# Order of the seven products in the mixer's pairs, decay rows loaded in twos, and the place of the SSD norm sums

## The chip, the cores and the metric

One Trainium2 chip, one core of it. The metric is the device time of one execution in microseconds, taken over several runs of the same program.

## The reference

One step of a one-layer streaming encoder over 512 prompt frames and 64 sample frames (576 columns in the kernel), width 1024, all in float32:

```python
def layer(x, lp, st):
    h = x + 0.5 * swiglu(rmsnorm(x, lp['norm_ffn1']), lp['w_ffn1_in'], lp['w_ffn1_out'])
    mix, new_st = mixer(rmsnorm(h, lp['norm_mix']), lp, st)
    h = h + mix
    h = h + 0.5 * swiglu(rmsnorm(h, lp['norm_ffn2']), lp['w_ffn2_in'], lp['w_ffn2_out'])
    return h, new_st

def mixer(u, lp, st):
    (z, xbc, dt_raw, aq, ak, av, mq, mk, mv, mo, mi, mf, gl) = split_cols(u @ lp['w_in'], IN_SIZES)
    ...   # SSD scan of 16 heads in 4 groups: decays from cumulative sums of dt * a; conv of width 4 before it
    y_ssd = rmsnorm(y.reshape(bsz, L, SSD_WIDTH).astype(u.dtype) * jax.nn.silu(z), lp['ssd_norm'])
    ...   # band attention of 8 heads; mLSTM of 4 heads with its own decay rows and stabiliser
    merged = (g_ssd * (y_ssd @ lp['w_proj_ssd']) + g_att * (y_att @ lp['w_proj_attn'])
              + g_ml * (y_ml @ lp['w_proj_mlstm']))
    return merged @ lp['w_out'], (k_new, v_new, ssd_new, conv_new, c_new, n_new, m_new)
```

The RMS norm of `y_ssd` needs the sum of squares over all 1024 SSD channels of a frame.

## The kernel before

The kernel has three parts: a first feed-forward part, the mixer, and a second feed-forward part. A large share of all weight columns is multiplied in pairs of column tiles: two 128-column tiles of a weight against the 1024 x 576 activations, the activations cut into four quarters and the weights into four blocks. A pair takes seven products of half depth instead of eight (a scheme of Strassen's kind). The products are named by their operands: X1, A11, X3, X4, A22, A21, X2. A product is 4 steps of depth, each with three matmuls of 288 columns (high part by high part, high by low, low by high: `product`, L500 to 506), so 12 matmuls on line 505. There are 91 pairs, 35 of them in the mixer.

`stationary` (L415) makes the seven weight operands of a pair. Four blocks come from memory: a pair of blocks `wx` on SyncE's queue, onto which a second load on GpSimd's queue adds (L431), and three blocks `wr`. GpSimd makes two sums more (`wy`: x3 on L434, x4 on L439). Each operand is then split into a high part on ScalarE (`ph`, L251) and the rest on VectorE (`pl`, L252). The rings hold 6 `ph`, 6 `pl`, 5 `wr`, 2 `wx` and 2 `wy`.

`pair` (L447, mixer) and `swiglu_unit` (L508, feed-forward) issue the products. In the mixer three PSUM banks serve all pairs, and the next pair starts one bank further (`pair_step` is 1), so its banks `pa`, `pb`, `pc` are this pair's `pb`, `pc`, `pa`. In `pair` X1, X3, A22 and X2 add up on `pa`, A11 stands alone on `pb`, X4 and A21 add up on `pc`. Partial results are read between products: `v` (after X1, L469), `u` (after X3, L474) and `m6` (after X4, L477) are copied by ScalarE into three `uv` tiles. The four results leave through `emit`: those of A11, A22 and A21 on VectorE (L462), that of X2 on ScalarE (L460), with the nonlinear function on ScalarE behind VectorE's (L464). The next product on a bank has to wait for the read before it.

In the mixer the loop of `branches` (L1186, over `ORDER`) goes through twelve units: four attention units `a`, four mLSTM units `m` and four SSD units `s`, in the order a0 a1 m0 s0 a2 a3 s1 m1 s2 m2 s3 m3. From the third unit on each first issues the pairs of its own input columns, then one or two pairs of gate columns (`merge_gates`), then its branch work (`attn`, `ml`, `ssd`).

The decay rows (24 rows of 576 in the scratch tensor `scr_rows`) are broadcast to all partitions by loads on ScalarE's queue into tiles 2 to 7 of `R1`, which `b()` (L144) hands out in turn. An mLSTM unit takes two: `nmB` (read early, L815, L833) and `eiB` (read until the last state update, L854). Half an SSD unit takes three: `cum[0]` and `cum[1]` (loaded on L958; read by L968, L971, L993, then turned into weights by L995 to L998) and `ec` (two loads of 64 partitions on L961, read late, L999 and L1035).

After the loop the sums of squares of the SSD outputs, gathered in `self.ss`, are totalled over partitions by matmuls (`total`, L277), raised to -1/2 on GpSimd (L269), spread by matmuls again (`spread`, L293) and copied to `rs` by ScalarE. `merge` (L1061) then projects attention, mLSTM and SSD outputs in this order; `rs` is used for the last of them.

Instructions are written in the source's order, but the framework places them on the five engines' queues itself: it keeps dependencies, and among what its own timing model calls ready it prefers what stands earlier in the source. Every queue then runs in order and waits by semaphores.

## Time and profile before

| what | us |
|---|---|
| median of 3 runs | 2030.58 |
| lowest and highest run | 2024.3 and 2036.96 |
| the profiled execution, whole | 2030.21 |
| the profiled execution, span from first to last instruction | 2028.4 |
| TensorE busy | 1941.9 |
| VectorE busy | 1363.5 |
| ScalarE busy | 1033.7 |
| GpSimd busy | 631.9 |

The mean granted clock of TensorE is 0.978 of full speed. Matmuls are pipelined, so that two or three records overlap and a busy TensorE need not be at its peak; the distance from one start to the next tells the pace. Loads and other DMA issues are instructions of the queue that issues them, but are not counted as busy.

### The profile page before, as it was taken

The page shows a single profiled execution, that of the slowest core. Times are in us where ns is not written, and L with a number is a line of the kernel's source. Part 1 is how long each engine was busy: PE and PEld are TensorE (multiplying, and loading weights), DVE is VectorE, ACT ScalarE, POOL GpSimd, SP SyncE. Part 2 cuts the span into 40 slices and gives each one's busy share as a digit, 9 for nine tenths or more (in the row PEclk, how much of TensorE's full clock was granted, in tenths as well). Part 3 has the DMA queues.
Part 4 walks back from the last instruction along what each step waited for, and adds up shares of the span by engine and source line. Part 5 has one row for each costly group of instructions (what it writes and reads, how often), then busy time and mean ns, then how long its engine had stood idle before and what let it go on. Part 6 is the DMA issues. An engine that isn't in the chain of part 4 may idle for free.

```text
span 2028.4 us, 37734 instructions
## 1 busy us (share of the span) xinstructions
PE 1941.9 (96%) x14177; PEld 1877.0 (93%) x14177; DVE 1363.5 (67%) x2475; ACT 1033.7 (51%) x2188; POOL 631.9 (31%) x626
## 2 busy tenths in 40 slices
PE   9899999999999889899897998899999999999998
PEld 8899999999999669779897898799999999999998
DVE  7866656666669867667676674565686666666665
ACT  4545444544545576766766755233554544454453
POOL 5223222232202234324434353261132322222221
PEclk9899999999999899999999999899999999999999
DMA  6345445544644435645656567562234644564441
GB/s 191 89 124 161 126 125 140 156 115 126 158 123 128 119 103 148 187 128 146 177 133 166 148 172 231 159 185 87 77 95 128 164 124 126 141 157 115 126 117 66
DMA packets 127840, 278.19 MB, mean 137 GB/s; under 512 B 14225, under 2 KB 26129, under 8 KB 127657
## 3 DMA queue, kind: packets, MB, share of 16 engines
q1 hardware_dynamic: 100648, 201.74, 30.3%
q0 software_dynamic: 16304, 59.52, 16.0%
q10 hardware_dynamic: 10704, 14.52, 2.5%
q8 instruction: 112, 1.84, 0.4%
q14 instruction: 72, 0.58, 0.1%
HBM read 255.16 MB, written 20.56 MB: 136 GB/s over the span
## 4 chain that ended last, share of the span: by engine, by line
PE 47%; DMA 5%; ACT 2%; POOL 2%; issue 2%; DVE 2%; POOLq 0%; DVEq 0%; ACTq 0%
PE acc L505 25%; PE acc L223 19%; DMA R<-scr_rows 2%; DMA wx<-in_sblk 2%; DMA y<-ys 1%; ACT ph L251 1%; PE ps_s L748 0%; DVE pl L252 0%; PE ps_v L759 0%; POOL R L997 0%; POOL wy L439 0%; PE ps_x L736 0%; PE ps_s L1008 0%; POOL wy L434 0%; ACT L464 0%
## 5 line engine op out<-in xcount | busy, mean ns | idle before, releaser
L505 PE MATMUL acc<-TH,ph 128*128 128x288 f32 x2548 | 768.7, 302 | 31.9 <-DVE g L462 9.7
L505 PE MATMUL acc<-TL,ph 128*128 128x288 f32 x2548 | 760.6, 299 | 3.4 <-DVE TL L252 3.4
L505 PE MATMUL acc<-TH,pl 128*128 128x288 f32 x2548 | 758.8, 298 | 0.4 <-DVE pl L252 0.4
L251 ACT CAST ph<-wr 128x512 fp32r<-128x512 f32 x495 | 306.3, 620 | 469.8 <-PE acc L223 202.3
L505 PEld LDWEIGHTS acc<-TH,ph 128*128 128x128 f32 x2548 | 484.0, 190 | 46.2 <-DVE g L462 11.7
L505 PEld LDWEIGHTS acc<-TH,pl 128*128 128x128 f32 x2548 | 485.8, 191 | 4.6 <-issue 3.9
L505 PEld LDWEIGHTS acc<-TL,ph 128*128 128x128 f32 x2548 | 485.3, 190 | 4.5 <-DVE TL L252 3.6
L223 PE MATMUL acc<-YH,ph 128*128 128x320 f32 (+1 forms) x1536 | 455.1, 298 | 9.3 <-ACT YH L251 4.5
L252 DVE TENSOR_TENSOR pl<-wr,ph 128x512 fp32r<-128x512 f32 x495 | 373.7, 756 | 133.5 <-ACT ph L251 122.6
L223 PE MATMUL acc<-YL,ph 128*128 128x320 f32 (+1 forms) x1536 | 455.8, 298 | 2.6 <-DVE YL L302 2.2
L223 PE MATMUL acc<-YH,pl 128*128 128x320 f32 (+1 forms) x1536 | 452.9, 297 | 0.0
L223 PEld LDWEIGHTS acc<-YH,ph 128*128 128x128 f32 x1536 | 292.1, 191 | 10.8 <-ACT YH L251 4.7
L223 PEld LDWEIGHTS acc<-YL,ph 128*128 128x128 f32 x1536 | 292.6, 191 | 4.3 <-DVE YL L302 3.1
L223 PEld LDWEIGHTS acc<-YH,pl 128*128 128x128 f32 x1536 | 291.8, 191 | 0.1
L434 POOL TENSOR_TENSOR wy<-wx,wr 128x512 f32<-128x512 f32 x91 | 127.3, 1399 | 494.1 <-DVE pl L252 172.1
L252 DVE TENSOR_TENSOR pl<-wx,ph 128x512 fp32r<-128x512 f32 x182 | 159.8, 879 | 54.6 <-ACT ph L251 51.4
L431 POOL DMA_DIRECT2D wx<-in_sblk x91 | 80.5, 888 | 351.8 <-DMA wx<-in_sblk 133.5
L252 DVE TENSOR_TENSOR pl<-wy,ph 128x512 fp32r<-128x512 f32 x182 | 144.5, 795 | 66.7 <-ACT ph L251 65.6
L566 DVE SCALAR_TENSOR_TENSOR R<-acc,R 128x256 f32<-128x256 f32 (+1 forms) x256 | 116.0, 453 | 90.4 <-PE acc L223 87.1
L251 ACT CAST ph<-wy 128x512 fp32r<-128x512 f32 x182 | 112.4, 619 | 122.4 <-PE acc L223 63.8
L251 ACT CAST ph<-wx 128x512 fp32r<-128x512 f32 x182 | 112.6, 619 | 110.1 <-PE acc L505 74.6
L439 POOL TENSOR_TENSOR wy<-wy,wr 128x512 f32<-128x512 f32 x91 | 136.1, 1495 | 30.8 <-DMA wr<-in_sblk 15.1
(296 smaller groups left out, 2255.9 us busy)
## 6 DMA issues: line engine op xcount, KB each, us to landing
wr<-in_sblk SPq DMA_DIRECT2D x273, 256.0 KB, 2.7
wr<-in_wblk SPq DMA_DIRECT2D x222, 256.0 KB, 3.1
wx<-in_sblk SPq DMA_DIRECT2D x91, 512.0 KB, 3.7
wx<-in_sblk POOLq DMA_DIRECT2D x91, 512.0 KB, 5.6
R<-scr_rows ACTq DMA_DIRECT2D x24, 288.0 KB, 4.5
gs<-g SPq DMA_DIRECT2D x24, 288.0 KB, 4.2
y<-gs POOLq DMA_DIRECT2D x24, 288.0 KB, 3.7
y<-ys POOLq DMA_DIRECT2D x16, 288.0 KB, 3.3
```

Of the source, the lines that this page charges most:

```text
L223: nc.tensor.matmul(ps[:, :n], wt[:, wsl], xx[:, k0 + k, a:a + n], start=(k == 0 and i == 0), stop=(k == nk - 1 and i == 2))
L251: self.nc.scalar.copy(hi, src)
L252: self.nc.vector.tensor_tensor(lo, src, hi.bitcast(F32), op=ALU.subtract)
L431: nc.gpsimd.dma_start(x12, src[:, 1:3, :], accum_op=ALU.add)
L434: nc.gpsimd.tensor_tensor(x3, x12[:, 0, :], a22, op=ALU.add)
L439: nc.gpsimd.tensor_tensor(x4, x3, a21, op=ALU.add)
L505: self.nc.tensor.matmul(ps, wt[:, wsl], xx[:, t, kk, :], start=(start and kk == 0 and i == 0), stop=(kk == 3 and i == 2), skip_group_check ...
L566: nc.vector.scalar_tensor_tensor(x[:, ot, sl], ps, 0.5, x[:, ot, sl], op0=ALU.mult, op1=ALU.add)
```

## The change

The diff has four parts.

- In `pair` the order of the products becomes X1, X4, then X2 of the pair before, X3, A21, A11, A22; X2 is kept as `open_pair` and issued by the next pair (or by `pair_end` before the last unit). `pa`, `pc`, `pb` are the first, second and third bank now. The operands are split in the order of `MUSE` in the mixer.
- `stationary` writes all loads first, then both sums, then the splits. In the feed-forward parts the order of the splits (`FUSE`) is the one of before; in the mixer the block for A11 is loaded last.
- `b()` hands out the six tiles in two groups of three and loads two rows with one DMA. An mLSTM unit leaves its third tile unused.
- The output DMA of the convolution rows (`co`), the totals of the SSD sums and their spread move from behind the loop to a place ahead of the last unit's branch work.

```diff
-    def b(self):
+    def b(self, step, r0):
+        i = 2 + self.b_i % 2 * 3
         self.b_i += 1
-        return self.R1[:, 2 + (self.b_i - 1) % 6, :]
+        self.nc.scalar.dma_start(self.R1[:, i:i + 2, :], self.rows(r0, 128, step))
+        return [self.R1[:, i + j, :] for j in range(3)]
...
+    FUSE = (T_X1, T_A11, T_X3, T_X4, T_A22, T_A21, T_X2)
+    MUSE = (T_X1, T_X4, T_X3, T_A21, T_A11, T_A22, T_X2)
...
         x12 = self.ring("wx", shape=(128, 2, 512))
         nc.sync.dma_start(x12, src[:, 0:2, :])
         nc.gpsimd.dma_start(x12, src[:, 1:3, :], accum_op=ALU.add)
-        a11, a22 = load(0), load(2)
-        x3 = self.ring("wy")
-        nc.gpsimd.tensor_tensor(x3, x12[:, 0, :], a22, op=ALU.add)
-        out[self.T_X1] = self.parts(x12[:, 0, :])
-        out[self.T_A11] = self.parts(a11)
-        a21 = load(3)
-        x4 = self.ring("wy")
-        nc.gpsimd.tensor_tensor(x4, x3, a21, op=ALU.add)
-        out[self.T_X3] = self.parts(x3)
...
+        for q in (2, 3, 0) if self.mixer else (0, 2, 3):
+            load(q)
+        raw["x3"] = add(x12[:, 0, :], raw[2])
+        raw["x4"] = add(raw["x3"], raw[3])
...
+        return {t: self.parts(at[t]) for t in (self.MUSE if self.mixer else self.FUSE)}
...
-        pa, pb, pc = self.pair_banks()
+        pa, pc, pb = self.pair_banks()
...
         self.product(pa, ops, self.T_X1, True)
-        v = tmp()
-        nc.scalar.activation(v, pa, AF.Copy, scale=s1)
+        v = tmp(pa, s1)
+        self.product(pc, ops, self.T_X4, True)
+        m6 = tmp(pc, s2)
+        self.pair_end()
+        self.product(pa, ops, self.T_X3, False)
+        u = tmp(pa, s2)
+        self.product(pc, ops, self.T_A21, False)
+        put2(1, H[1], emit(pc, s2, u, ALU.subtract))
         self.product(pb, ops, self.T_A11, True)
         put1(1, H[1], emit(pb, s1, v, ALU.add))
-        self.product(pa, ops, self.T_X3, False)
-        u = tmp()
-        nc.scalar.activation(u, pa, AF.Copy, scale=s2)
-        self.product(pc, ops, self.T_X4, True)
-        m6 = tmp()
-        nc.scalar.activation(m6, pc, AF.Copy, scale=s2)
         self.product(pa, ops, self.T_A22, False)
         put2(0, H[0], emit(pa, -s2, m6, ALU.add))
-        self.product(pc, ops, self.T_A21, False)
-        put2(1, H[1], emit(pc, s2, u, ALU.subtract))
-        self.product(pa, ops, self.T_X2, False)
-        put1(0, H[0], emit(pa, s1))
+
+        def end():
+            self.product(pa, ops, self.T_X2, False)
+            put1(0, H[0], emit(pa, s1))
+        self.open_pair = end
+
+    def pair_end(self):
+        end, self.open_pair = self.open_pair, None
+        if end:
+            end()
...
-    def rows(self, r0, n):
-        return bass.AP(self.scr.tensor, self.scr.offset + r0 * T, [[0, n], [1, T]])
+    def rows(self, r0, n, step=0):
+        return bass.AP(self.scr.tensor, self.scr.offset + r0 * T, [[0, n]] + [[step * T, 2]] * bool(step) + [[1, T]])
...
-        nmB, eiB = self.b(), self.b()
-        nc.scalar.dma_start(nmB, self.rows(16 + h, 128))
-        nc.scalar.dma_start(eiB, self.rows(20 + h, 128))
+        nmB, eiB, _ = self.b(4, 16 + h)
...
-            cum = [self.b(), self.b()]
-            for r in range(2):
-                nc.scalar.dma_start(cum[r], self.rows(d0 + r, 128))
-            ec = self.b()
+            *cum, ec = self.b(1, d0)
...
+                if n == len(ORDER) - 1:
+                    self.pair_end()
+                    nc.sync.dma_start(self.O["co"], self.co)
+                    for (a, m), acc in zip(HALVES, self.ss):
+                        pt = self.ps("x")
+                        self.total([acc], m, pt)
+                        nc.scalar.copy(self.rs[:, a:a + m], self.spread(pt, m)[0][:, :m])
                 units[u[0]][1](u[1], t)
                 if n == GATES:
                     self.gates(pre)
-            nc.sync.dma_start(self.O["co"], self.co)
-            for (a, n), acc in zip(HALVES, self.ss):
-                pt = self.ps("x")
-                self.total([acc], n, pt)
-                nc.scalar.copy(self.rs[:, a:a + n], self.spread(pt, n)[0][:, :n])
```

## Rows read from the trace of the kernel before

**Rows 1.** The page: its first line, and shares of the chain that ended last.

```profile
span 2028.4 us, 37734 instructions
...
PE acc L505 25%; PE acc L223 19%; DMA R<-scr_rows 2%; DMA wx<-in_sblk 2%; DMA y<-ys 1%; ACT ph L251 1%; PE ps_s L748 0%; DVE pl L252 0%; PE ps_v L759 0%; POOL R L997 0%; POOL wy L439 0%; PE ps_x L736 0%; PE ps_s L1008 0%; POOL wy L434 0%; ACT L464 0%
```

**Rows 2.** Busy time by stage: from:to length, per engine busy us (instructions), clock, DMA.

```profile
core 0: us, PE busy (x) PEld busy (x) DVE busy (x) ACT busy (x) POOL busy (x), PEclk, DMA share, GB/s
100.00:600.00 500.00, 500.00 (x3759) 500.00 (x3758) 320.96 (x537) 227.41 (x436) 125.06 (x105) 1.00 0.51 138
640.00:1257.00 617.00, 564.82 (x3991) 508.62 (x3991) 436.41 (x907) 411.64 (x985) 245.46 (x258) 0.96 0.56 152
1257.00:1294.00 37.00, 24.00 (x108) 20.50 (x108) 14.21 (x33) 10.12 (x29) 11.98 (x21) 0.68 0.58 186
...
1530.00:2000.00 470.00, 470.00 (x3537) 469.95 (x3536) 300.85 (x486) 208.52 (x396) 115.57 (x98) 1.00 0.47 128
```

**Rows 3.** TensorE's waits, 640 to 1257: us, times, longest us.

```profile
PE acc L505 <- DVE g L462: 9.7, 4, 3.7
PE acc L505 <- ACT g L460: 8.9, 3, 5.5
PE acc L505 <- ACT uv L474: 4.5, 4, 3.6
...
PE acc L505 <- ACT P L460: 2.0, 1, 2.0
```

**Rows 4.** Busy time, as rows 2, of two stretches at the lower clock.

```profile
1280.00:1291.40 11.40, 6.51 (x26) 6.33 (x27) 3.21 (x10) 1.66 (x3) 5.24 (x9) 0.50 0.53 180
1030.50:1033.90 3.40, 3.40 (x17) 3.40 (x16) 3.40 (x11) 2.12 (x6) 0.73 (x2) 0.50 0.45 154
```

**Rows 5.** ScalarE in order of time, 1240 to 1249: start, us, what.

```profile
1240.08 0.40 ACT L477 ACTIVATE uv<-acc 128x288 f32<-128x288 f32 x1
...
1243.26 0.40 ACT L469 ACTIVATE uv<-acc 128x288 f32<-128x288 f32 x1
...
1246.85 0.40 ACT L460 ACTIVATE g<-acc 128x288 f32<-128x288 f32 x1
...
1248.49 0.41 ACT L474 ACTIVATE uv<-acc 128x288 f32<-128x288 f32 x1
```

**Rows 6.** VectorE in order of time, 1241 to 1246.

```profile
1241.30 0.46 DVE L462 SCALAR_TENSOR_TENSOR g<-acc,uv 128x288 f32<-128x288 f32 x1
...
1244.86 0.46 DVE L462 SCALAR_TENSOR_TENSOR g<-acc,uv 128x288 f32<-128x288 f32 x1 [0.78 <-PE acc L505]
```

**Rows 7.** Pieces of the chain that ended last, in order of time: start, us.

```profile
820.33 1.60 PE acc L505 x12
...
1102.43 4.88 DMA R<-scr_rows
```

**Rows 8.** ScalarE and its queue in order of time, 1096 to 1117.

```profile
1096.22 0.33 ACTq L958 DMA_DIRECT2D R<-scr_rows  x1
...
1102.43 0.32 ACTq L958 DMA_DIRECT2D R<-scr_rows  x1
...
1115.67 0.40 ACT L460 ACTIVATE g<-acc 128x288 f32<-128x288 f32 x1
```

**Rows 9.** DMA issues, 640 to 1300: count, KB each, median us to landing.

```profile
wr<-in_sblk SPq DMA_DIRECT2D x99, 256.0 KB, 3.0
wx<-in_sblk SPq DMA_DIRECT2D x35, 512.0 KB, 3.6
```

**Rows 10.** GpSimd in order of time, at 1253, with the idle time before it.

```profile
1253.36 0.89 POOL L431 DMA_DIRECT2D wx<-in_sblk  x1 [8.38 <-DVE pl L252]
```

**Rows 11.** VectorE at 1133 and GpSimd at 1174, in order of time.

```profile
1133.73 0.34 DVE L854 SCALAR_TENSOR_TENSOR cs<-cs,R,ps_s 128x129 f32<-128x129 f32 x1
...
1174.74 6.39 POOL L997 TENSOR_TENSOR R<-R,t 128x512 f32<-128x512 f32 x4
```

**Rows 12.** TensorE in order of time, 1280 to 1292.

```profile
1280.18 1.01 PE L277 MATMUL ps_x<-ones,sumsq 128*128 128x1 f32 x4 [0.53 <-DVE g L884]
...
1291.44 1.05 PE L293 MATMUL ps_x<-ident,sm 128*128 128x128 f32 x4
```

More of the change, by code (lines that the diff above doesn't have):

```diff
@@ L77, in __init__ @@
         self.b_i = 0
+        self.open_pair = None
         nc = self.nc
@@ L421, in stationary, with add @@
         src = self.I["sblk"][i].rearrange("p (q c) -> p q c", q=4)
+        raw = {}
         def load(q):
-            w = self.ring("wr")
-            nc.sync.dma_start(w, src[:, q, :])
-            return w
-        out = {}
+            raw[q] = self.ring("wr")
+            nc.sync.dma_start(raw[q], src[:, q, :])
+        def add(one, two):
+            o = self.ring("wy")
+            nc.gpsimd.tensor_tensor(o, one, two, op=ALU.add)
+            return o
         x12 = self.ring("wx", shape=(128, 2, 512))
@@ L431, in stationary @@
         nc.gpsimd.dma_start(x12, src[:, 1:3, :], accum_op=ALU.add)
[L432 to L445 removed]
+        for q in (2, 3, 0) if self.mixer else (0, 2, 3):
+            load(q)
+        raw["x3"] = add(x12[:, 0, :], raw[2])
+        raw["x4"] = add(raw["x3"], raw[3])
+        at = {self.T_X1: x12[:, 0, :], self.T_X2: x12[:, 1, :], self.T_X3: raw["x3"], self.T_X4: raw["x4"],
+              self.T_A11: raw[0], self.T_A22: raw[2], self.T_A21: raw[3]}
+        return {t: self.parts(at[t]) for t in (self.MUSE if self.mixer else self.FUSE)}
     def pair(self, one, two):
@@ L452, in pair, with tmp @@
         ops = self.stationary((name, c1, c2))
-        pa, pb, pc = self.pair_banks()
+        pa, pc, pb = self.pair_banks()
         H = (slice(0, FH), slice(FH, T))
-        tmp = lambda: self.gp.tile([128, FH], F32, name="uv", tag="uv", bufs=3)
+        def tmp(ps, scale):
+            o = self.gp.tile([128, FH], F32, name="uv", tag="uv", bufs=3)
+            nc.scalar.activation(o, ps, AF.Copy, scale=scale)
+            return o
         def emit(ps, scale, other=None, op=None):
```

5 lines of the change are left out of this document (removed).

## The prediction

> **What bounds the kernel now.** I read the busy time by stage first. In the feed-forward parts TensorE is busy every microsecond (500.00 of 500.00, 470.00 of 470.00) at full clock; nothing that the change does to weights or copies there can be seen unless it makes TensorE wait. The mixer, 640 to 1257 us, is different: 564.82 of 617.00 us busy, and the clock was granted at 0.96 on average. Behind it, 1257 to 1294, TensorE works 24 of 37 us at a clock of 0.68, since the last mLSTM unit ends there alone [rows 2]. So about 52 us of idle time and a few per cent of clock in the mixer are the stock that the change can draw on. Of this, the waits of product matmuls (L505) for a copy out of PSUM are, in their four largest rows, 9.7 + 8.9 + 4.5 + 2.0 = 25.1 us in 12 waits, the longest 5.5 us [rows 3]. After five of these waits the clock fell to 1.2 GHz for some 3.4 us; one stands, 0.50 over 3.40 us [rows 4]. Each such stretch costs half of itself, 1.7 us, together 8.5 us. The other waits of the mixer belong to the branches (softmax, states, norms), which the change does not touch.
>
> The chain that ended last names, beside products, the loads of the decay rows: 2% of the span [rows 1].
>
> **Which order runs today.** The new order shall put more work between a copy and the product that needs its bank. Whether it does depends on the order that runs, and that is not the order of the source. The source puts X2 of a pair before X1 of the next. On ScalarE, however, the copy of X4 (L477, 1240.08) is followed by that of the next pair's X1 (L469, 1243.26), and only then by that of X2 (L460, 1246.85) and of the next X3 (L474, 1248.49) [rows 5]. Between them lie on VectorE the copies of A22 (1241.30) and A21 (1244.86) [rows 6]; A21 adds onto X4's bank and so can't have run before that bank's copy had ended at 1240.48 and 1.60 us more had gone by. So TensorE runs X4, A22, X1', A21, X2, X3', A11', X4', A22': the next pair's first product has already been pulled forward. This is so at 29 of the 34 borders of two mixer pairs (L469 of the next before L460 of this one), of which the border in [rows 5] is the last. Counted on the three banks, every copy there has two products behind which to hide: X1 to X3 (A21, X2), X3 to A22 (A11, X4), X4 to A21 (A22, X1'), A22 to X2 (X1', A21), and X2, A21 and A11 to the next user of their bank likewise. The new source order X1, X4, X2 of the pair before, X3, A21, A11, A22 gives each copy two products as well. A product is 12 matmuls in 1.60 us [rows 7], so the cover is 3.2 us before and after.
>
> **The change part by part.**
> *Interleave.* Same 35 pairs, same seven products, same copies, same weight splits. Gain at the usual borders: none; at the five others one product of cover at most, 1.60 us each. Bounds: 0 and 22 us (the first rival). I take 0, by [rows 5, 6], the rows nearest to it. The first weight sum now needed early (X4 second) is no new wait so long as GpSimd keeps its lead; the splits run through the same six buffers. The moved X2 keeps its split two products longer, which leaves A22 of the next pair a lead of three products, 4.8 us. In the feed-forward parts only the order in which weight work is written changes; TensorE's full stages hide it, and without that cover it would cost at most a product per stage.
> *Decay rows.* Twelve loads of 288 KB fewer, as many bytes. Each issue takes ScalarE's queue 0.33 us [rows 8], 4 us in all, hidden since ScalarE is busy 411.64 of 617.00 us [rows 2]. Twice the bytes land later: 3.0 us for 256 KB and 3.6 us for 512 KB [rows 9], so the first row comes 0.6 us later. The gain is where the second row was asked for late. In the last SSD unit the loads were issued at 1096.22 and 1102.43, the second took 4.88 us on the chain [rows 7, 8], and ScalarE, late by this and by table loads, reached the copy L460 only at 1115.67 [rows 8]: this is the longest wait of all, 5.5 us [rows 3], and it dropped the clock. One load brings the second row 6.21 - 0.6 = 5.6 us sooner. That ends the wait and its slow stretch: 5.5 + 1.7 = 7.2 us. There is a catch in the buffers. Groups of three make the second half of an SSD unit behind an mLSTM unit load its rows into the two buffers of that unit, whose second one is read until the last state update (L854, 1133.73), while today only the late-needed third tile waits for it. The load moves some 30 us later there; its product on GpSimd (L997) starts at 1174.74 [rows 11], so this is hidden, and it too takes ScalarE's work out of the crowd at 1102 to 1116. If the crowd forms again elsewhere, the gain is 0. I take 7.2.
> The row says that 256 KB more cost 0.6 us. The Trainium skill, DMA: Bandwidth & Descriptors, section Anatomy of one DMA, gives every DMA a fixed part of about 2.0 us beside its bytes; if all twelve saved loads stood on the path, that would be an estimate of 24 us, 2007 us in the end. The traces here show no such path but the case above; this result is weighed among the rivals.
> *Norm sums.* Twenty small matmuls leave the end. There four of L277 took 1.01 us and four of L293 1.05 us [rows 12], at half clock (0.50 from 1280 to 1291.4 [rows 4]), so 0.13 us each at full clock, 2.6 us for twenty. Most of them ran while TensorE waited for the last unit anyway; only about 1.1 us stood among the merge's matmuls. In their new place they lie among products: +2.6 - 1.1 = +1.5 us. The output DMA of the convolution rows moves along on SyncE's queue, one issue, hidden. After the last pair X2 now follows A22 at once and waits for its copy, 0.46 us long [rows 6]; this falls into time that the last unit leaves free.
>
> Sum, against the profiled execution's 2030.2 us (span 2028.4 [rows 1] and 1.8 around it; the median of the runs is 0.4 above): 0 - 7.2 + 1.5 = -5.7, so 2024.5; I say 2024 us.
>
> **The rivals.**
> *The interleave works.* If the order that runs gains a whole product of cover, each wait loses up to 1.60 us: 6.4 of the 9.7 (four waits), 4.8 of the 8.9 (three), 1.6 + 0.9 of the 4.5 (longest 3.6), 1.6 of the 2.0, together 15.3 us [rows 3]; four of five slow stretches go with it, 6.8 us. With what is left of the row loads' 7.2 (3.9) and +1.5 this is 2030.2 - 22.1 - 3.9 + 1.5 = 2006 us. For it: five borders still run in the poor order, and the placing then no longer hangs on guesses. Against: the two-product cover of [rows 5, 6].
> *The loads are the path.* 2% of the span is 40.6 us [rows 1]; half of the loads gone would take 20.3: 2030.2 - 20.3 + 1.5 = 2011 us. Against: twins that were issued together already overlap, and the consumers are ScalarE and VectorE, not TensorE.
> *The norm sums stall the products.* The sums need a power on GpSimd, and TensorE's queue then holds matmuls that wait for it, with products queued behind them and, behind these, every copy. GpSimd stood 8.38 us before a weight load in just this stretch [rows 10]. If the power is queued behind such a wait, once for each half, TensorE loses up to 16.8 us and two slow stretches, 3.4: 2024.5 + 20.2 = 2045 us. It makes the kernel slower than before once both waits together pass 5.7 us. For it: GpSimd's queue is in order and waits for transfers; against: nothing needs these sums at once, so they can be placed late.
> *Nothing moves.* ScalarE's crowd forms elsewhere and the sums cost little: 2030 us.
>
> **How the numbers follow.** My forecast (2014 to 2034) 0.42; the interleave works 0.26; the loads are the path 0.08; the norm sums stall 0.14; nothing 0.10. The likeliest is 2024 us. Faster by over 1% (below 2010; about 1% is what a measurement of this kernel can tell from no change) has the 0.26 and half of 0.08: 0.30. Slower by over 1% (above 2051) has the far end of the third rival: 0.06. Within: 0.64. Leaving out the lowest part of the first rival and the highest of the third, the range is 2003 to 2044 us.
>
> **What would show it.** Right: the sum of the L505 waits for copies falls by about the one long wait and not by half; ScalarE's order shows the copies of X1, X4, X2, X3 in a row; the decay rows are 12 loads of 576 KB that land in 5 us or so; the second load of the last SSD unit lies after the last state update. Wrong: L505 waits under 12 us and clock stretches gone (first rival), TensorE waiting at L293 for GpSimd between 1220 and 1257 (third). A weight split for A22 or X4 as releaser of a product would mean that the lead I counted as enough is not.

## The result, and the profile after

The changed kernel takes 2037.22 us in the median of 20 runs (2029.76 to 2046.3), the kernel before 2033.16 us in as many runs beside it (2024.3 to 2039.28). The ratio is 1.0027, with a 95% interval of 1.0015 to 1.0039: by this about 5.5 us slower, where 6 us faster had been forecast. The profiled execution has a span of 2034.0 us, against 2028.4 us [rows 1].

The first line of the page after, and busy time by stage (columns as in [rows 2]):

```profile
span 2034.0 us, 37661 instructions
```

```profile
core 0: us, PE busy (x) PEld busy (x) DVE busy (x) ACT busy (x) POOL busy (x), PEclk, DMA share, GB/s
640.00:1257.00 617.00, 561.17 (x3928) 504.19 (x3927) 427.50 (x899) 410.38 (x978) 239.56 (x256) 0.95 0.55 150
1257.00:1294.00 37.00, 22.82 (x144) 20.25 (x142) 16.76 (x34) 13.25 (x35) 11.61 (x18) 0.78 0.61 177
```

Within the same 617 us the mixer issued 3928 matmuls instead of 3991 [rows 2]. TensorE is busy 3.65 us less, and its mean clock is 0.95 instead of 0.96. The last matmul of the mixer's products starts at 1265.9 us instead of 1256.8 (rows of the product's line), so the loss is made in the mixer. The feed-forward parts were not the place: by the rows of the product the first one runs 1.6 us ahead of before from its fourth pair to its end, and the second one 5.4 to 5.5 us behind from its fourth pair to its end.

TensorE's waits for a copy, after, from 640 to 1257 (us, times, longest; L523 is the product's line now, L465 copies v, u and m6, L471 and L473 are the results on ScalarE and VectorE):

```profile
PE acc L523 <- ACT uv L465: 14.6, 9, 5.3
PE acc L523 <- ACT g L471: 6.7, 3, 4.5
PE acc L523 <- DVE g L473: 3.9, 4, 2.0
PE acc L523 <- DVE R L473: 1.2, 2, 0.6
```

These four are 26.4 us in 18 waits. Before, the product's waits for copies were 25.1 us in the four largest rows [rows 3] and 27.2 us in all. So the interleave did not take the waits away, but it did not add to them either.

ScalarE in order of time, after: four copies in the new order X1, X4, X2 of the pair before, X3, as the source has them.

```profile
1224.28 0.41 ACT L465 ACTIVATE uv<-acc 128x288 f32<-128x288 f32 x1
1225.88 0.40 ACT L465 ACTIVATE uv<-acc 128x288 f32<-128x288 f32 x1
...
1232.66 0.40 ACT L471 ACTIVATE g<-acc 128x288 f32<-128x288 f32 x1
1233.84 0.41 ACT L465 ACTIVATE uv<-acc 128x288 f32<-128x288 f32 x1
```

Before, the second of these places was held by VectorE's copy of A21, and X4 was sixth [rows 5, 6]. The decay rows come as planned (DMA issues, 640 to 1257: count, size, median us to landing):

```profile
R<-scr_rows ACTq DMA_DIRECT2D x12, 576.0 KB, 5.9
```

To see where the time goes, the mixer is cut in two in all kernels below: from the first matmul of its products to the last one, and from there to the 97th matmul of the merge (start to start), when in these two kernels all branch work is done. Idle is time with no matmul in flight; the last column but one is the time in the first stretch in which the records of the granted clock show 0.5.

| kernel | first to last product, us | idle in it | of it at 1.2 GHz | last product to the merge's 97th matmul |
|---|---|---|---|---|
| before | 612.7 | 52.2 | 44.4 | 42.9 |
| after | 623.3 | 55.8 | 61.4 | 41.4 |

After loses 10.6 us among the products: 3.6 us more idle, and 17 us more at half speed, which cost up to half of themselves, 8.5 us (the two overlap in part). At the end it gains 1.5 us. One execution of each stands behind these figures, and executions of one kernel differ by several us (the kernel before took 2017.64 to 2038.36 us in one set of 32 runs). Verdicts therefore rest on the ratios over many runs, and the traces only say where to look.

### The profile page after: what moved, and what is told of

It is laid out like the page before. It is cut to its first block, busy times and chain, and to the rows that moved or that the text cites. A ratio compares the mean times of both kernels' runs of the same rounds, so it can differ in the third digit from the quotient of the medians.

```text
span 2034.0 us, 37661 instructions
## 1 busy us (share of the span) xinstructions
PE 1940.2 (95%) x14177; PEld 1875.7 (92%) x14177; DVE 1360.7 (67%) x2475; ACT 1036.9 (51%) x2190; POOL 628.8 (31%) x626
## 3 DMA queue, kind: packets, MB, share of 16 engines
q0 software_dynamic: 16304, 59.52, 16.1%
## 5 line engine op out<-in xcount | busy, mean ns | idle before, releaser
L523 PE MATMUL acc<-TH,ph 128*128 128x288 f32 x2548 | 773.0, 304 | 29.2 <-ACT uv L465 14.6
L523 PE MATMUL acc<-TL,ph 128*128 128x288 f32 x2548 | 762.3, 299 | 3.4 <-DVE TL L256 3.4
L523 PE MATMUL acc<-TH,pl 128*128 128x288 f32 x2548 | 761.6, 299 | 0.0
L523 PEld LDWEIGHTS acc<-TH,ph 128*128 128x128 f32 x2548 | 486.5, 191 | 42.1 <-ACT uv L465 17.3
L523 PEld LDWEIGHTS acc<-TL,ph 128*128 128x128 f32 x2548 | 487.4, 191 | 5.5 <-DVE TL L256 3.6
L523 PEld LDWEIGHTS acc<-TH,pl 128*128 128x128 f32 x2548 | 488.1, 192 | 2.9 <-issue 2.2
L438 POOL TENSOR_TENSOR wy<-wy,wr 128x512 f32<-128x512 f32 x91 | 134.8, 1481 | 34.6 <-DMA wr<-in_sblk 14.8
```

The source lines that it names most:

```text
L438: nc.gpsimd.tensor_tensor(o, one, two, op=ALU.add)
L523: self.nc.tensor.matmul(ps, wt[:, wsl], xx[:, t, kk, :], start=(start and kk == 0 and i == 0), stop=(kk == 3 and i == 2), skip_group_check ...
```

## The experiments

### Each part by itself

Four kernels, each the kernel before with one part of the change. The interleave:

```diff
+    MUSE = (T_X1, T_X4, T_X3, T_A21, T_A11, T_A22, T_X2)
...
-        pa, pb, pc = self.pair_banks()
+        pa, pc, pb = self.pair_banks()
...
+        self.product(pc, ops, self.T_X4, True)
+        m6 = tmp(pc, s2)
+        self.pair_end()
```

> The kernel before with the new order of the seven products, the pair left open, and the new stationary operands; rows loaded one at a time and norm sums at the end as before. Theory A (the steps of the prediction; the order that ran before already gave every copy two products, and the loss of the changed kernel is the norm sums): no change, within 3 us of before, waits of products for copies near 27 us in the mixer. Theory B (the new order of loads and weight sums delays GpSimd's SSD work and the weights, and this is where the changed kernel lost its 10 us in pairs 57 to 62): 5 to 10 us slower. Theory C (the interleave gives each wait a product of cover, and the other parts ate this up): 10 us or more faster, copy waits under 12 us.

Measured: ratio 1.0029 (1.0016 to 1.0042), 5.9 us slower. Copy waits are 25.8 us, as theory A had it, but the time is not the same: from first to last product 626.1 us, 57.6 idle, 78.5 us of it at 1.2 GHz. Theory B gave the size; that its mechanism is the cause is not shown by this.

The rows:

```diff
-        return self.R1[:, 2 + (self.b_i - 1) % 6, :]
+        self.nc.scalar.dma_start(self.R1[:, i:i + 2, :], self.rows(r0, 128, step))
```

> The kernel before with the decay rows two per load in groups of three tiles, nothing else. Theory A: 7 us faster, since the longest wait of all (5.5 us at 1116 us, a copy on ScalarE behind the decay-row work of the last SSD unit) and its slow stretch go. Theory B: no change within 2 us; the copy is late for another reason than the second row's load and the wait of 5 us or so stays (the changed kernel has one of 5.6 us at the same place). Theory D (groups of three make row loads wait for the tile before): 3 us or more slower.

Measured: ratio 0.9954 (0.9936 to 0.9971), 9.3 us faster. That is theory A's size. But the wait that theory A was to remove is still there, and this is looked into below.

The norm sums, with the store of the convolution rows:

```diff
+                if n == len(ORDER) - 1:
+                    nc.sync.dma_start(self.O["co"], self.co)
+                    for (a, m), acc in zip(HALVES, self.ss):
+                        pt = self.ps("x")
+                        self.total([acc], m, pt)
```

> The kernel before with the store of the convolution rows and the norm sums moved ahead of the last unit, nothing else. Theory A as predicted: 1.5 us slower. Theory A as it stands after the result (the sums hold both PSUM tiles that the last unit's transposes need, and its store comes 9 us later): 6 to 10 us slower, with the transposes of the last unit at 1250 us or later in place of 1237 to 1243. Theory B: within 1.5 us, the last unit where it was.

Measured: ratio 1.0015 (1.0001 to 1.0030), 3 us slower: between 0.2 and 6 us, so the 1.5 us of the prediction are in, 6 to 10 us hardly. The last unit's store does come later, at 1287.40 us instead of 1280.35.

The weight loads and sums written first, in the old order of products:

```diff
+        for q in (0, 2, 3):
+            load(q)
+        raw["x3"] = add(x12[:, 0, :], raw[2])
+        raw["x4"] = add(raw["x3"], raw[3])
```

> The kernel before with the weight loads and sums written first in both the feed-forward parts and the mixer, in the old order of products and splits. Theory A: no change within 1.5 us; the first pair some 1.1 us earlier and the stall of 1.7 us at 1516 us may go, as in the changed kernel, so up to 3 us faster. Theory E (any rewriting lets the framework place the mixer's instructions anew, and this alone moves the time by 5 us either way): a change of 3 us or more with a different set of waits in the mixer.

Measured: ratio 1.0009 (0.9994 to 1.0024), no difference that can be told. This also answers theory E in part: a rewriting that lets the framework place instructions anew need not move the time.

The parts alone add up to 5.9 - 9.3 + 3.0 = -0.4 us (the interleave contains the rewritten loads); the whole is +5.5. Each of these figures is uncertain by some 3 us either way, so that they do not simply add is likely rather than certain. The interleave is the one with the largest price.

### What the interleave costs, and which part of it

First the changed kernel without the moved norm sums:

```diff
-                    for (a, m), acc in zip(HALVES, self.ss):
-                        pt = self.ps("x")
...
+            nc.sync.dma_start(self.O["co"], self.co)
+            for (a, n), acc in zip(HALVES, self.ss):
```

> The changed kernel without the move of the convolution rows' store and the norm sums (both behind the loop again); interleave and rows two per load stay. Theory N (the norm sums hold the PSUM tiles of the last unit's transposes and cost the changed kernel its 9 us): the store of the last unit falls back to 1280 us or sooner, 2025 us or less. Theory I (the interleave alone delays the last unit as far, and the sums add little): 2033 to 2039 us, as the interleave alone.

Measured: ratio 1.0015 (1.0000 to 1.0029). By the middle values the sums account for 0.0012, 2.4 us of the changed kernel's loss, though the two intervals overlap; theory N's 9 us are out. Then the changed kernel without the interleave:

```diff
-        self.product(pc, ops, self.T_X4, True)
-        m6 = tmp(pc, s2)
-        self.pair_end()
+        self.product(pb, ops, self.T_A11, True)
+        put1(1, H[1], emit(pb, s1, v, ALU.add))
```

> The changed kernel without the interleave: rows two per load, norm sums and store of the convolution rows moved, weight loads written first, the old order of products. Theory L (parts add up: rows -9, sums +3, the rest 0 to +2): 4 to 6 us faster than before. Theory O (rows gained by the place of the last unit on TensorE's queue, and here no product stands behind its state matmuls, as in the kernel before): no gain, 0 to 6 us slower than before.

Measured: ratio 0.9977 (0.9965 to 0.9989), 4.7 us faster than before, as adding up the parts gave it, and against theory O. With the interleave the same kernel stands at 1.0027. So the interleave costs 0.0050 in the whole, 10 us.

Is it the open pair, or the order? The order that ran before [rows 5, 6] also interleaves two pairs, but X4 is its sixth product. So this kernel writes just that order down, nothing else changed:

```diff
         self.product(pa, ops, self.T_X1, True)
         v = tmp(pa, s1)
+        self.pair_end()
         self.product(pa, ops, self.T_X3, False)
         u = tmp(pa, s2)
         self.product(pb, ops, self.T_A11, True)
         put1(1, H[1], emit(pb, s1, v, ALU.add))
         self.product(pc, ops, self.T_X4, True)
         m6 = tmp(pc, s2)
         self.product(pa, ops, self.T_A22, False)
         put2(0, H[0], emit(pa, -s2, m6, ALU.add))
+        def end():
+            self.product(pc, ops, self.T_A21, False)
+            put2(1, H[1], emit(pc, s2, u, ALU.subtract))
+            self.product(pa, ops, self.T_X2, False)
+            put1(0, H[0], emit(pa, s1))
+        self.open_pair = end
```

> The kernel before with another interleave, written in the order that already ran there: X1, then the last two products A21 and X2 of the pair before, X3, A11, X4, A22; operands split in this order, loads as before, rows one per load, norm sums at the end. Two products of cover for every copy here too, but the sums x3 and x4 of GpSimd are needed third and sixth, not fourth and second. Theory Q (the interleave of the change costs its 6 us because X4 stands second: ScalarE and GpSimd then wait for the weight sums and their accumulating load with copies queued behind; ScalarE's waits for wy and wx were 19.9 us there, 5.1 before): within 3 us of before, these waits under 9 us. Theory A2 (leaving a product open across pairs costs by itself, as the store of the last unit comes later): 4 us or more slower than before.

Measured: ratio 0.9993 (0.9979 to 1.0007), as before, and 0.0036 (7 us) below the interleave of the change. TensorE's waits for copies in it, 640 to 1257:

```profile
PE acc L519 <- ACT uv L461: 5.7, 6, 2.1
PE acc L519 <- ACT g L467: 5.5, 3, 2.0
PE acc L519 <- DVE R L469: 1.6, 2, 1.3
PE acc L519 <- DVE P L469: 1.5, 2, 0.8
PE acc L519 <- DVE g L469: 1.0, 1, 1.0
PE acc L519 <- ACT P L467: 0.8, 1, 0.8
```

16.1 us instead of 27.2: an interleave can shorten these waits, if it stands in this order. The time did not follow in this kernel, since waits of branch matmuls grew from 24.5 to 30.3 us and the time at 1.2 GHz from 44.4 to 61.4. One point of theory Q failed here, and it is the mechanism: ScalarE's waits for weights and their sums were to fall under 9 us and are 20.5 (18.3 for the accumulated load, 2.2 for GpSimd's sums), as many as with the interleave of the change (19.9).

Two more pairs of kernels differ in nothing but this order. The changed kernel in the order as it ran:

```diff
-        pa, pc, pb = self.pair_banks()
+        pa, pb, pc = self.pair_banks()
...
-        self.product(pc, ops, self.T_X4, True)
-        m6 = tmp(pc, s2)
         self.pair_end()
```

> The changed kernel with nothing but the order of its products altered: X1, A21 and X2 of the pair before, X3, A11, X4, A22 in place of X1, X4, X2 of the pair before, X3, A21, A11, A22 (weight loads and splits in this order). Theory Q (X4 as second product is what the interleave costs, 6 us alone and 10 in the whole): 8 to 13 us faster than the changed kernel, so 3 to 8 us faster than before. Theory A2 (keeping products open across pairs costs): within 3 us of the changed kernel.

Measured: ratio 0.9950 (0.9934 to 0.9965), 10 us faster than before and 0.0077, 15.6 us, faster than the changed kernel. And the best kernel (rows two per load, the last unit's branch work first, see below) in either order; this edit puts the last unit first:

```diff
-                    self.merge_gates(n - 2)
-                    if n - 2 >= len(ORDER) - 4:
+                    if n < len(ORDER) - 1:
+                        self.merge_gates(n - 2)
+                    if n - 2 >= len(ORDER) - 4 and n < len(ORDER) - 1:
                         self.merge_gates(n)
...
                 units[u[0]][1](u[1], t)
+                if n == len(ORDER) - 1:
+                    self.merge_gates(n - 2)
+                    self.merge_gates(n)
+                    self.pair_end()
```

> The interleave in the order that already ran, rows two per load, last unit's branch work ahead of its gate pairs, norm sums at the end. Theory Q with O: 5 to 12 us faster than before. Theory A2: no better than before.

> The best kernel so far (the order as it ran, rows two per load, last unit's branch work first: 0.990 of before) with only the order of products altered to that of the change, X4 second and X2 alone open. Theory Q: 7 to 12 us slower than it, so 8 to 13 us faster than before. Theory A2: no slower than it.

Measured: 0.9901 (0.9880 to 0.9922) in the order as it ran, 2012.28 us in the median; 0.9990 (0.9976 to 1.0003) with X4 second. The difference is 0.0089, 18 us. Theory Q had the sign each time and too small a size in the last three kernels: 8 to 13 us expected and 15.6 measured, 5 to 12 and 20, 7 to 12 and 18, so that the last kernel is only 2 us below before instead of 8 to 13. Theory A2 is out: keeping products open across pairs costs nothing by itself. Three times the order alone decides, and in no pair do the two intervals touch. (The order here is the whole of it, with the loads and splits that go with it; no run moves X4 alone.)

| kernel | order | ratio | first to last product | idle in it | at 1.2 GHz |
|---|---|---|---|---|---|
| interleave alone | X4 second | 1.0029 | 626.1 | 57.6 | 78.5 |
| | as it ran | 0.9993 | 610.3 | 46.7 | 61.4 |
| whole change | X4 second | 1.0027 | 623.3 | 55.8 | 61.4 |
| | as it ran | 0.9950 | 602.3 | 45.9 | 23.9 |
| rows, last unit first | X4 second | 0.9990 | 628.9 | 58.2 | 68.3 |
| | as it ran | 0.9901 | 609.5 | 47.2 | 37.5 |

Each time some 10 us of idle time and 17 to 38 us at half speed go. In each pair the products' waits for copies (640 to 1257) are shorter as well, although the cover, as written, is two products in both orders: 16.1 us instead of 25.8, 20.2 instead of 26.4, 21.8 instead of 28.1.

Why the copies come later with X4 second is not settled by these traces. The first suspect is GpSimd, whose sum x4 is needed earlier. GpSimd's waits ahead of its weight sums (us, times, longest), first the changed kernel, then the same kernel in the order as it ran:

```profile
POOL wy L438 <- DVE pl L256: 62.5, 13, 6.9
POOL wy L438 <- issue: 29.9, 6, 7.3
...
POOL wy L438 <- DMA wx<-in_sblk: 5.6, 1, 5.6
```

```profile
POOL wy L437 <- DMA wx<-in_sblk: 72.7, 15, 7.3
POOL wy L437 <- DVE pl L256: 19.1, 4, 10.9
...
POOL wy L437 <- issue: 15.3, 3, 6.5
```

By the names, the sums of the second kernel start when their weights land, and those of the first when VectorE has split an operand and so set a buffer free. The names divide the kernels by order without exception: 15, 14, 15 and 17 waits for the load in the kernel before and the three with the order as it ran; one or none in the three with X4 second. But a wait for several things is named after one of them only, and the landing times in the trace say otherwise. One of the sums of the changed kernel, with the load that it needs:

```profile
651.18 0.92 POOL L443 DMA_DIRECT2D wx<-in_sblk  x1 [1.50 <-DVE ga L645]
...
658.03 1.32 POOL L438 TENSOR_TENSOR wy<-wx,wr 128x512 f32<-128x512 f32 x1 [3.24 <-DVE pl L256]
```

The load landed at 657.90; the split that the wait is named after had ended at 657.54. Of the 35 first sums (x3) of the mixer's pairs, 32 start within 0.25 us behind the landing of their own load in the changed kernel, 31 in the same kernel in the order as it ran, 30 in the kernel before. So GpSimd starts on the load in either order, and that it lost a lead, or that its two `wy` tiles hold it up, is not shown. ScalarE's waits for weights do not part the orders either: with X4 second and as it ran they are 19.9 and 20.5 us, 17.1 and 16.7, 15.9 and 17.9 in the three pairs of the table. Only the part of them that is for GpSimd's sums is larger with X4 second: 12.6, 6.5 and 7.1 us against 2.2, 2.3 and 2.8.

How a late weight can reach a product is seen at 1195 us of the changed kernel. GpSimd in order of time, then ScalarE, then TensorE:

```profile
1177.48 6.41 POOL L1010 TENSOR_TENSOR R<-R,t 128x512 f32<-128x512 f32 x4
1183.86 2.05 POOL L1011 TENSOR_TENSOR R<-R,t 64x64 f32<-64x64 f32 x4
1185.86 0.85 POOL L443 DMA_DIRECT2D wx<-in_sblk  x1
1186.48 1.31 POOL L997 TENSOR_TENSOR t<-t,wd 128x512 f32<-128x512 f32 x1
1195.05 1.27 POOL L438 TENSOR_TENSOR wy<-wx,wr 128x512 f32<-128x512 f32 x1 [7.26 <-issue]
```

```profile
1195.01 0.62 ACT L255 CAST ph<-wx 128x512 fp32r<-128x512 f32 x1 [9.12 <-DMA wx<-in_sblk]
1195.53 0.40 ACT L471 ACTIVATE g<-acc 128x288 f32<-128x288 f32 x1
```

```profile
1195.99 0.61 PE L523 MATMUL acc<-TH,ph 128*128 128x288 f32 x1 [4.47 <-ACT g L471]
```

The accumulating load is issued behind 8.5 us of branch work on GpSimd (L1010, L1011) and lands 9.1 us later. ScalarE stands 9.12 us at the split that needs it, the copy L471 stands behind the split, and the product behind the copy. The product's wait is named after the copy, but the 3.2 us of two products could not hide it. This is one of the changed kernel's eight waits of a product of 1 us or more, 4.5 of their 21.4 us. The longest, 5.33 us at 1117.54, stands behind table loads and decay work on ScalarE, and the one of 3.66 us at 988.89 behind a late decay row. Nor is it a place where the order loses: in the order as it ran ScalarE stands 5.21 us at 1176.14 for the load of the same pair, and over the 84 matmuls around it that kernel's lead goes from 14.8 to 13.2 us. The changed kernel falls behind it at many places: by 7.5 us after eight such stretches of 84 matmuls, 17.2 after 18, 21.0 at the end. That the order is the cause is shown by the three pairs; which of its waits carries it stays open. A kernel with X4 alone moved, and one with a third `wy` tile, were not tried.

### What the rows two per load gained

The wait at 1116 us was to go. In the kernel with rows alone it is there, 5.60 us at 1114.56. ScalarE ahead of it:

```profile
1104.37 1.28 ACT L467 ACT_TABLE_LOAD   x1 [1.83 <-DVE wd L967]
...
1106.63 1.28 ACT L969 ACT_TABLE_LOAD   x1
1107.93 0.21 ACT L969 ACTIVATE el<-R 128x4 f32<-128x4 f32 x1
...
1108.44 1.28 ACT L467 ACT_TABLE_LOAD   x1
...
1110.18 1.28 ACT L971 ACT_TABLE_LOAD   x1
...
1111.59 1.50 ACT L991 ACTIVATE R<-R,TM 128x128 f32<-128x128 f32 x5
...
1114.12 0.39 ACT L477 ACTIVATE uv<-acc 128x288 f32<-128x288 f32 x1
```

Four table loads, 5.1 us, as ScalarE changes between the gate function of the results (L467) and the exponentials of the decay work (L969 and after). The same four stand there before: 1107.65, 1109.41, 1111.44 and 1113.19. The page ScalarE activation tables: per-element evaluation and per-set limits of the Trainium skill (section What a function is on this engine) puts two functions of different sets one such load of 1283 ns apart; the trace agrees, 1283 ns each. To see whether they are the cause, the kernel before, with rows one per load, and with ScalarE copying where the pairs have a gate function:

```diff
             def go(dst, a=0, b=FH, func=None):
+                func = func and AF.Copy
```

> The kernel before with the gate and sigmoid functions of the mixer's pairs left out: ScalarE copies in their place, with as many instructions of the same shape, so that it need not change its function table between them and the exponentials of the branches (46 table loads of 1.28 us in the mixer before). Theory T (the longest wait of a product, 5.5 us at 1116 us, is four table loads in a row on ScalarE, 5.1 us, ahead of the copy that the product needs; the second decay row is not what it waits for): that wait falls under 1.5 us with the rows loaded as before, and the kernel is more than 10 us faster. Theory R (the wait is the late second row's load): the wait stays above 4 us.

Measured: ratio 0.9933 (0.9909 to 0.9958), 13.6 us faster. Table loads between 640 and 1257 fall from 46 to 11, and the product's waits are short everywhere (us, times, longest):

```profile
PE acc L506 <- DVE g L463: 5.1, 5, 2.1
PE acc L506 <- ACT uv L470: 4.2, 3, 2.8
PE acc L506 <- ACT uv L475: 4.1, 5, 2.0
```

No wait of a product of 1.3 us or more lies between 1070 and 1200. Theory T is right: the wait was the table loads', not the late row's. (A branch matmul waits 4.9 us for GpSimd at 1120 instead.)

Where, then, do the 9 us come from? In the trace of rows alone the products take 5.4 us more (618.1), and the end 32.0 us instead of 42.9. The last mLSTM unit stands otherwise on TensorE's queue: its first state matmul has four products behind it, in the kernel before none. Its output is stored at 1273.57 instead of 1280.35 (SyncE's row of the store), and the merge waits for it. So two kernels asked whether the loads or this place made the gain. Groups of three tiles with one row per load:

```diff
-        self.nc.scalar.dma_start(self.R1[:, i:i + 2, :], self.rows(r0, 128, step))
+        for r in range(2):
+            self.nc.scalar.dma_start(self.R1[:, i + r, :], self.rows(r0 + r * step, 128))
```

> The kernel before with the tiles of the decay rows handed out in groups of three as in the change, but with one row per load (24 loads of 288 KB, as before). Theory L (the gain of rows alone is that of fewer, larger loads): no change from before. Theory O (the gain comes from where the framework then places the last unit's matmuls on TensorE's queue, which hangs on anything written differently): the time moves by the store of the last mLSTM unit, end = store + 746 us within 2 us, wherever that store falls; a gain as large as that of rows alone would mean the groups matter and not the loads.

Measured: ratio 1.0032 (1.0017 to 1.0046), 6.5 us slower; idle time among the products 62.4 us, a single wait for a copy 8.88 us. The store falls at 1288.04. Theory L had expected no change, so it missed the price of the groups; the end of the execution comes 748.9 us behind the store, against 748.0 in the kernel before, so theory O's link between the two holds, with a constant 2 to 3 us larger than it said. And two per load in the mLSTM units alone:

```diff
-        for r in range(2):
-            self.nc.scalar.dma_start(self.R1[:, i + r, :], self.rows(r0 + r * step, 128))
+        if step == 4:
+            self.nc.scalar.dma_start(self.R1[:, i:i + 2, :], self.rows(r0, 128, step))
+        else:
+            for r in range(2):
+                self.nc.scalar.dma_start(self.R1[:, i + r, :], self.rows(r0 + r * step, 128))
```

> Groups of three tiles as in the change; two rows per load only in the four mLSTM units, the last unit among them; one row per load in the SSD units (20 loads). On TensorE's queue the last unit stands as in the kernel before, with no product behind its states. Theory L (the last unit ends sooner since its two rows come with one load): 5 us or more faster than groups of three with single rows, so no slower than before. Theory O: as groups of three with single rows, 3 to 10 us slower than before, store at 1284 us or later.

Measured: ratio 0.9992 (0.9976 to 1.0008), 8 us faster than groups with single rows. The last unit stands as before, so theory O fails for this gain: it was made among the products (609.0 us, 51.1 idle; groups with single rows 621.1 and 62.4). Its store falls at 1274.11, where theory O had 1284 or later. Theory L gave the size, though by its mechanism the gain would stand at the end, which is 42.3 us against 43.4. So the groups cost some 6 us when the rows come singly, and loads of two give this back; the further step to rows alone shows at the end.

### The place of the last unit

The branch work of the last unit written ahead of its gate pairs (the diff stands above; `pair_end` only where a pair is open), in the kernel before, in the changed kernel, and with rows alone:

> The kernel before with one edit: the branch work of the last mLSTM unit is written ahead of its two pairs of gate columns instead of behind them; nothing of the change is in it. On TensorE's queue the unit's first state matmul then has 8.7 products behind it, in the kernel before none, with rows two per load alone 4. Theory O (what decides is where the last unit's matmuls stand among the last products): its store falls at 1270 us or sooner (before: 1280.4) and the kernel is 8 to 14 us faster than before. Theory L (fewer, larger row loads made the gain of rows alone; nothing of them is here): no gain. Rival W (TensorE then waits for the unit's copies with fewer products as cover): within 3 us or slower.

> The changed kernel with the same edit, the last unit's branch work ahead of its two pairs of gate columns (8.8 products behind its first state matmul; the changed kernel has none). Theory O: store at 1270 us or sooner (changed kernel: 1289.7), 10 to 16 us faster than the changed kernel, so 5 to 10 us faster than before. Theory P (the products in the mixer are slower by the interleave and this remains): at most 4 us faster than the changed kernel.

> The kernel before with rows two per load and with the last unit's branch work written ahead of its gate pairs; nothing else. Theory O: both put the last unit's matmuls ahead of products (here 9.6 of them behind its first state matmul, 4 with rows alone), so the gains do not add: 5 to 10 us faster than before. Theory L (a gain of the loads, 9 us, and one of the place, 6 us): 13 us or more faster.

Measured: 0.9971 (0.9948 to 0.9993), 5.9 us faster than before; 1.0019 (1.0001 to 1.0038), within 2 us of the changed kernel; 0.9960 (0.9944 to 0.9975), no more than rows alone. The end shrinks each time, to 30.3, 28.0 and 29.9 us. In the kernel before this is the gain, smaller than the 8 to 14 us expected; its store falls at 1261.02, as theory O said, and some of the unit's matmuls now lie among the products, which take 4.5 us more. With rows two per load it is a gain that rows alone had made already, so theory O is right about the end and about the sum. In the changed kernel theory O failed and theory P's size came: the end shrinks by 13.4 us, but the store still falls at 1286.03, and the products took 639.9 us in the profiled run, its slowest (2041.22, median 2034.58). There the norm sums show what they can do (TensorE's waits, 1230 to 1262):

```profile
PE ps_x L297 <- POOL sm L273: 4.9, 1, 4.9
PE ps_x L281 <- DVE sumsq L267: 2.4, 1, 2.4
```

TensorE stands 4.9 us before the spread, waiting for GpSimd's power, with products queued behind. That is the mechanism of the prediction's third rival. In the changed kernel itself only the wait for the sums (2.5 us at 1232.76) shows.

The same end from the other side: the merge loads and projects the attention outputs first, so that the gate loads no longer stand on GpSimd's queue behind the load of the last unit's output.

```diff
-        for i in range(8):
-            self.split(load(self.ys[i]), YH[:, i, :], YL[:, i, :])
         for branch, w in ((1, "w_proj_attn"), (2, "w_proj_mlstm")):
+            for i in range(4 * branch - 4, 4 * branch):
+                self.split(load(self.ys[i]), YH[:, i, :], YL[:, i, :])
```

> The changed kernel, with one edit in the merge: it loads and splits the four attention outputs, projects them, and only then loads the four mLSTM outputs (before: all eight first, so that on GpSimd's queue the gate loads of the attention part stand behind the load of the last mLSTM unit's output). Theory S (the end follows the last mLSTM unit's store, 9.4 us later in the changed kernel than before, and this is where its time went): from the merge's first matmul (1272.3 us) to its 48th (1300.6 us) lie 28.3 us; 6.4 of it are those matmuls and some 3 the last unit's own, so 15 to 19 us faster than the changed kernel, near 2020 us. Theory P (the products before the merge are what got slower, and the store is late as a consequence only): under 4 us faster.

> The kernel before with rows two per load, and the same edit in the merge. Theory S: rows alone gained 9 us since its last unit's store came 6.8 us sooner; with the store off the path 48 matmuls of the merge, which took 17.4 us there, take 6.4 and some 2 of the last unit: another 7 to 9 us, near 2013 us. Theory P: within 3 us of rows alone (2021 us).

Measured: the changed kernel goes from 1.0027 to 0.9962 (0.9945 to 0.9978), 13 us; rows alone stays, 0.9949 (0.9934 to 0.9964) against 0.9954. In both the merge then waits 6.0 and 6.4 us ahead of its mLSTM part, for outputs that are now loaded late, which gives back a part. So theory S holds for the changed kernel, where the late store was most of what stood in the merge's way, with 2 us less than it said; for rows alone, whose store was early already, theory P's size came, and what was won at the merge's start was lost again at its mLSTM part.

## Why the prediction was right or wrong

**The bound.** Right. What the change did, it did in the mixer and at its end; the forecast's stock of idle time and slow clock was the place of the gains and of the loss.

**The order that ran.** Right as a count. Two products covered a copy before and after, and waits for copies went from 27.2 to 26.4 us. What does not follow from the count is an equal time, as the next point shows. The bound kept open for the interleave, up to 22 us of gain, was no fancy either: written in the order that had run, copy waits fell to 16.1 us, and together with rows and the last unit's place the kernel reached 0.9901.

**The interleave at 0: the step that failed.** The interleave was entered with 0, because every copy keeps two products of cover, and with the sentence that a weight sum needed early "is no new wait so long as GpSimd keeps its lead". The term measured +5.9 us alone and +10 us in the whole (1.0027 against 0.9977). The mistake was to take equal cover for equal time: two orders with the same cover of two products differ by 7, 15.6 and 18 us in three pairs of kernels, and the waits for copies in them by 6 to 10 us. Products were moved, and so were the times at which their operands must be ready and their copies taken: X4 from sixth to second place is four products or 6.4 us earlier [rows 7], for an operand that takes an accumulating load, two sums and a split. No price was put on this. That GpSimd lost its lead by it is not shown, since its first sums start on the landing of their load in either order (32 and 31 of 35), so through which wait the order costs its time stays open.

**The slow clock.** The forecast charged each wait its half-speed stretch, and this was right in kind: of the 10.6 us lost among the products up to 8.5 are clock. But it charged the product's waits alone. Waits of branch matmuls were left out, as work that the change does not touch, and those grew from 24.5 to 29.0 us.

**Decay rows.** Right in sign and, alone, in size (-7.2 forecast, -9.3 measured, interval -13.0 to -5.9); wrong in mechanism. The wait of 5.5 us was four table loads; it outlived the change (5.3 us at 1117.54 there). The working had named table loads beside the late row and then given the whole wait to the row. The gain came elsewhere: loads of two gave back what the groups cost with single rows, and the rest shows at the end, with the last unit's other place. With the interleave in place it was 0.0014 (1.0029 to 1.0015), 3 us, with intervals that overlap. The load's size was about right: 576 KB land in 5.9 us, 288 KB in 4.5 before (24 loads). The fixed part of the Trainium skill's DMA: Bandwidth & Descriptors, section Anatomy of one DMA, which that section gives for loads that GpSimd issues, would make an estimate of 24 us over twelve loads; no run here shows that for these loads on ScalarE's queue.

**Norm sums.** +1.5 us forecast, +2.4 in the whole and +3.0 alone (0.2 to 6.1). Right in sign, low by a us or so: TensorE's wait for the sums was not in the working.

**The sum.** 0 - 7.2 + 1.5 became, as it added in the whole, +10 for the interleave and -4.7 for all the rest (1.0027 and 0.9977). One term, entered as nothing, turned the sign. The measured 2037 us lies in the range, since that reached to 2044 for the third rival; the mechanism that took it there was for the most part not the one for which that end was kept, so that was luck.

**What was to show it.** The copies stood in a row as forecast; the loads are 12 of 576 KB; the second load of the last SSD unit is issued at 1139.86, behind the last state update at 1139.13. The last tell, a weight split as releaser of a product, did not show. It could have been missed by its name: at 1195 us a split held up ScalarE's queue, and the product's wait bore the copy's name.

## What to carry to other kernels

When work is reordered to hide a result's copy, equal cover is not equal time: list for every moved step when its operands must be ready as well as when its results are read, and run a second order with the same cover beside it. The name of a wait's releaser is a lead and not a cause: hold the start of the instruction against the landing of its load before the name is believed. A wait for a copy on an engine that also splits weights, or changes function tables, is priced by reading back along that engine's queue. Where a framework places the instructions, the order that ran is the first version to write down, and a gain of one part is to be measured in the whole.

## What the runs showed of the hardware

- The accumulating load of 512 KB on GpSimd's queue lands in 6.1 us (median of 35), the plain one of the same size on SyncE's queue in 3.6 us [rows 9]; one accumulating load above took 9.1. No run parts the accumulation from the queue.
- Executions of one kernel on one chip differ by up to 1% with no change of instructions: 2017.64 to 2038.36 us over 32 runs of the kernel before. Rows alone was much steadier, 2020.57 to 2023.06 in six runs; why is open.
- A few us of idle time cost more than themselves: in the whole change the order that saved 9.9 us of idle time between first and last product also saved 37.5 us at 1.2 GHz, up to 18.8 us of work (one execution of each).
